# The cosine product of the rotated heads gets a tile of its own

## The chip, the cores and the metric

The kernel runs on one core of a Trainium2 chip. What counts is the device time of one execution in microseconds (us). The kernel before was timed three times: median 1780.94 us, lowest 1780.46, highest 1782.49. The execution that was profiled took 1781.29 us, of which 1779.5 us are the profile's span.

## The reference

Two layers of an encoder over 512 tokens and 1024 channels, all in float32. Each layer runs three token mixers side by side (differential attention, a convolution module, a neighbourhood attention), merges them through gates, and adds a feed-forward part and a gated input embedding. The change lies in the differential attention, whose queries and keys are first turned by a rotary embedding:

```python
def apply_rope(x, cos, sin):
    half = x.shape[-1] // 2
    x1, x2 = x[..., :half], x[..., half:]
    rot = jnp.concatenate([-x2, x1], axis=-1)
    return (x.astype(jnp.float32) * cos + rot.astype(jnp.float32) * sin).astype(x.dtype)

# diff_attention, 4 heads of 2 x 64 channels
q = apply_rope(q, cos, sin)
k = apply_rope(k, cos, sin)
s = jnp.einsum('bhcqd,bhckd->bhcqk', qi, k).astype(f32) * scale
a = jax.nn.softmax(s, axis=-1)
a = (a[:, :, 0] - lam * a[:, :, 1]).astype(v.dtype)
o = jnp.einsum('bhqk,bhkd->bhqd', a, v)
```

## The kernel before

Channels lie on the 128 partitions, the 512 tokens along the free axis. Every float32 product is made of three TensorE (PE) products of a high and a low part: ScalarE (ACT) copies an operand to the high part, VectorE (DVE) subtracts it to get the low part (`split`; its two instructions stand at L143 and L157, the lines of the helpers `act` and `tt`). Weights come as 512 KB tiles by transfers that SyncE (SP) issues (L171), and are split the same way into tiles `wh` and `wl`.

A stage is named by the first word of a tile: `natten` the neighbourhood attention, `diff` the differential attention, `gatec` the gates that are projected between its heads, `conv` the convolution, whose 31 taps per channel block (L160, tile `conv_z`) are slipped into DVE's order one by one after given instructions (`background`).

In the differential attention `diff_in` runs once for each of four heads, and in it once for the query (s=0) and once for the key (s=1). PE projects the head into PSUM. ACT copies it to a tile `raw`. Four transfers (L814) on SP's queue copy `raw` to a tile `rot` with the two halves of each 64 channels exchanged. DVE multiplies `raw` by the cosine table in place, `rot` by the sine table in place (whose sign is folded in), and adds. The sum is split: the high part goes to `kh`, the low part to `raw` itself, seen as another type. Transfers at L664 then stack both parts on partitions for the score products (`stack`). `raw` and `rot` both come from the pool tag `rp`, and both show as `diff_rp` in the profile; the cosine and sine tables show as `diff_r`. One convolution tap follows the cosine product (`bg["diff"]` is 1).

The scores of one head come in four units of 128 queries (`diff_unit`, `probs`). Each unit makes two score tiles `sc` in PSUM, one for each half of the differential head, each by two matmuls at L796. For each, DVE takes the maximum (L888) and ACT the exponential (into a tile `a` for the first, `e` for the second). There are two PSUM buffers for `sc`, so the second score tile of a unit can be written only when the exponential of the second tile of the unit before has been taken. I call the two score tiles of a unit a pair. The first pair of head 0 lies near 168 us of the span in the first layer and near 1049 us in the second.

PE's order is written out by the program. The order of the other engines' instructions (DVE, ACT, SP and the rest) is set by a scheduler when the kernel is built: it places each instruction where it expects its operands to be ready, and each engine then runs its list strictly in order, an instruction that waits holding up all that stand behind it.

## Time and profile before

| | |
|---|---|
| median of 3 runs | 1780.94 us (1780.46 to 1782.49) |
| profiled execution | 1781.29 us, span 1779.5 us |
| PE busy | 1764.2 us, 99% of the span |
| DVE busy | 1362.5 us, 77% |
| ACT busy | 900.6 us, 51% |
| transfers on SP's queue (q1) | 227.83 MB, 41.8% of 16 engines' span |

The views used below: the page; the waits (who waited for whom); the chain of waits, which is followed back from the last instruction and printed in order of time as start, duration, what; the timeline of one engine (start, duration, engine, line, operation, tile written <- tiles read, and in square brackets the idle time ahead of the instruction with what ended it); the groups by line (busy time, mean ns of one, idle time ahead with its cause); and the table of windows, which gives the busy time of each engine and the clock granted to PE in a stretch of the span. In the timeline a matmul's duration overlaps the next one's; how fast PE goes is read from the distance of starts.

### The profile page before, as it was taken

The numbers are of one execution on the slowest core, as the hardware profiler recorded it, in microseconds if no ns is written. First come the engines' busy times: TensorE is split into PE (matmuls) and PEld (weight loads), VectorE is DVE, ScalarE is ACT, GpSimd is POOL, SyncE is SP. The second block draws the span as 40 slices with busy tenths as digits, with TensorE's granted clock in tenths as the row PEclk, the third lists the DMA queues.
The fourth block names the chain that finished last, engine by engine and source line by source line (L and its number), as shares of the span: only waits on it lengthen the run. The fifth ranks groups of instructions, "written<-read, shape, count | busy, mean of one in ns | idle before, by whom it ended". The sixth has DMA issues, their size and how long they took to land.

```text
span 1779.5 us, 27113 instructions
## 1 busy us (share of the span) xinstructions
PE 1764.2 (99%) x10146; PEld 1555.6 (87%) x10146; DVE 1362.5 (77%) x2220; ACT 900.6 (51%) x1559; POOL 103.8 (6%) x114
## 2 busy tenths in 40 slices
PE   9999999999999999999999999999999999999998
PEld 7888888888899899998888888888888998989987
DVE  7867887998787576777776678889887865766676
ACT  5566545325576254454545655452356652634544
POOL 0000000000121010100000000000001210101000
PEclk9999999999999999999999999999999999999999
DMA  6575541334767365543536645423256664655332
GB/s 231 157 196 148 156 126 43 112 98 144 225 158 184 116 164 155 141 120 127 159 126 171 194 133 148 113 71 95 94 177 197 173 177 113 175 140 154 99 104 95
DMA packets 114787, 253.95 MB, mean 143 GB/s; under 512 B 16864, under 2 KB 23776, under 8 KB 114656
## 3 DMA queue, kind: packets, MB, share of 16 engines
q1 hardware_dynamic: 101264, 227.83, 41.8%
q0 software_dynamic: 12672, 23.07, 7.9%
q8 instruction: 80, 1.31, 0.3%
q10 hardware_dynamic: 720, 1.31, 0.2%
q14 instruction: 51, 0.42, 0.1%
HBM read 215.46 MB, written 7.34 MB: 125 GB/s over the span
## 4 chain that ended last, share of the span: by engine, by line
PE 92%; ACT 3%; DVE 2%; DMA 2%; issue 1%; SPq 0%; POOL 0%; ACTq 0%; POOLq 0%; DVEq 0%
PE ffn_mm L177 4%; PE ffn_mm L178 4%; PE ffn_mm L179 4%; PE ffn_mm L1005 3%; PE ffn_mm L1003 3%; PE ffn_mm L1004 3%; PE ffn_sc L1003 3%; PE ffn_sc L1004 3%; PE ffn_sc L1005 3%; PE mergea_mm L178 2%; PE mergea_mm L177 2%; PE mergea_mm L179 2%; PE gateb_mm L178 2%; PE gateb_mm L177 2%; PE gateb_mm L179 2%; PE wo_mm L177 2%
## 5 line engine op out<-in xcount | busy, mean ns | idle before, releaser
L160 DVE SCALAR_TENSOR_TENSOR conv_z<-glu_z,pre_par,conv_z 128x512 f32<-128x512 f32 x240 | 179.6, 748 | 3.4
L143 ACT ACTIVATE ffn_wh<-ffn_wr 128x1024 fp32r<-128x1024 f32 (+1 forms) x92 | 93.4, 1021 | 141.2 <-PE ffn_mm L178 76.0
L157 DVE TENSOR_TENSOR ffn_wl<-ffn_wr,ffn_wh 128x1024 fp32r<-128x1024 f32 (+1 forms) x92 | 107.6, 1175 | 41.2 <-ACT ffn_wh L143 40.9
L973 POOL DMA_DIRECT2D ffn_qk<-w_fu x88 | 77.8, 963 | 601.6 <-DMA ffn_qk<-w_fu 266.2
L157 DVE TENSOR_TENSOR ffn_t<-ffn_mm,wo_rb 128x512 f32<-128x512 f32 (+1 forms) x86 | 47.8, 557 | 71.7 <-PE ffn_mm L179 61.4
L143 ACT ACTIVATE mergea_wh<-mergea_wr 128x1024 fp32r<-128x1024 f32 (+1 forms) x32 | 27.1, 846 | 96.8 <-PE mergea_mm L178 79.5
L157 DVE TENSOR_TENSOR ffn_wl<-ffn_qk,ffn_wh 128x1024 fp32r<-128x1024 f32 x44 | 53.9, 1224 | 15.2 <-ACT ffn_wh L143 15.2
L143 ACT ACTIVATE ffn_wh<-ffn_qk 128x1024 fp32r<-128x1024 f32 x44 | 46.6, 1059 | 33.0 <-PE ffn_mm L178 16.2
L143 ACT ACTIVATE diff_a<-diff_sc,diff_s 128x512 f32<-128x512 f32 x32 | 21.9, 685 | 59.9 <-DVE diff_s L888 59.9
L177 PE MATMUL ffn_mm<-ffn_v,ffn_wh 128*128 128x512 f32 x132 | 51.4, 389 | 0.0
L178 PE MATMUL ffn_mm<-ffn_v,ffn_wh 128*128 128x512 f32 x132 | 51.4, 389 | 0.0
L179 PE MATMUL ffn_mm<-ffn_v,ffn_wl 128*128 128x512 f32 x132 | 51.3, 389 | 0.0
L177 PE MATMUL ffn_mm<-ffn_y,ffn_wh 128*128 128x512 f32 x132 | 51.3, 389 | 0.0
L178 PE MATMUL ffn_mm<-ffn_y,ffn_wh 128*128 128x512 f32 x132 | 51.3, 389 | 0.0
L179 PE MATMUL ffn_mm<-ffn_y,ffn_wl 128*128 128x512 f32 x132 | 51.3, 389 | 0.0
L1003 PE MATMUL ffn_mm<-wo_h,ffn_wh 128*128 128x256 f32 x176 | 49.9, 284 | 0.0
L1004 PE MATMUL ffn_sc<-wo_h,ffn_wh 128*128 128x256 f32 x176 | 49.8, 283 | 0.0
L1005 PE MATMUL ffn_mm<-wo_h,ffn_wl 128*128 128x256 f32 x176 | 49.8, 283 | 0.0
L1005 PE MATMUL ffn_sc<-wo_h,ffn_wl 128*128 128x256 f32 x176 | 49.8, 283 | 0.0
L1003 PE MATMUL ffn_sc<-wo_h,ffn_wh 128*128 128x256 f32 x176 | 49.8, 283 | 0.0
L1004 PE MATMUL ffn_mm<-wo_h,ffn_wh 128*128 128x256 f32 x176 | 49.8, 283 | 0.0
L143 ACT ACTIVATE natten_wh<-natten_wr 128x1024 fp32r<-128x1024 f32 x24 | 25.4, 1058 | 42.1 <-issue 15.2
(861 smaller groups left out, 6490.7 us busy)
## 6 DMA issues: line engine op xcount, KB each, us to landing
ffn_qk<-w_fu POOLq DMA_DIRECT2D x88, 256.0 KB, 6.2
ffn_wr<-w_fg SPq DMA_DIRECT2D x44, 512.0 KB, 4.8
ffn_wr<-w_fd SPq DMA_DIRECT2D x32, 448.0 KB, 4.1
ffn_r<-w_fu SPq DMA_DIRECT2D x44, 256.0 KB, 3.3
ffn_qk<-w_fg SPq DMA_DIRECT2D x44, 256.0 KB, 2.9
ffn_qk<-w_fu SPq DMA_DIRECT2D x44, 256.0 KB, 3.2
natten_wr<-w_in SPq DMA_DIRECT2D x16, 512.0 KB, 4.4
diff_wr<-w_in SPq DMA_DIRECT2D x16, 512.0 KB, 3.8
```

The source lines that it names most:

```text
L143: i = self.nc.scalar.activation(out, in_, func, **kw)
L157: return self.nc.vector.tensor_tensor(out, a, b, op)
L160: return self.nc.vector.scalar_tensor_tensor(out, a, s, b, op0, op1)
L177: mm(out, wh, ah, start=first, stop=False, **kw)
L178: mm(out, wh, al, start=False, stop=False, **kw)
L179: mm(out, wl, ah, start=False, stop=last, **kw)
L973: nc.gpsimd.dma_start(q, wu[:, lo], accum_op=ALU.add)
L1003: mm(out, wh[:, c], bh, start=first and k == 0, stop=False, skip_group_check=True)
L1004: mm(out, wh[:, c], bl, start=False, stop=False, skip_group_check=True)
L1005: mm(out, wl[:, c], bh, start=False, stop=k == 3, skip_group_check=True)
```

## The change

The cosine product is written to a new tile `t` from the pool tag `t` (seven buffers, used by other stages too) and no longer over `raw`. The sum is made in `t`, and the split reads `t`. The low part still goes to `raw`.

```diff
             for b in range(4):
                 o = b ^ 1
                 self.nc.sync.dma_start(rot[32 * b:32 * b + 32], raw[32 * o:32 * o + 32])
-            self.background(self.tt(raw, raw, st["tabs"][0], ALU.mult), self.bg["diff"])
+            t = self.sb("t", [P, 512])
+            self.background(self.tt(t, raw, st["tabs"][0], ALU.mult), self.bg["diff"])
             self.tt(rot, rot, st["tabs"][1], ALU.mult)
-            self.tt(raw, raw, rot, ALU.add)
+            self.tt(t, t, rot, ALU.add)
             nat, low = self.sb("kh", [P, 512], F32R), raw.bitcast(F32R)
-            self.split(nat, low, raw)
+            self.split(nat, low, t)
             self.stack(nat, low, st4[:, 2 * s:2 * s + 2], k2 if s else None)
```

The number of instructions and transfers stays as it was. The lists of PE and GpSimd (POOL) are the same before and after; those of DVE, ACT and SP differ inside the differential stage, in the same way in both layers. Because the diff adds a line, L888 is L889 in the changed kernel, and L893 is L894. The number at the end of a tile's name only tells instances apart.

DVE, first layer, query of head 1, in the kernel before (`diff_rp_1742` is `raw`, `diff_rp_1743` is `rot`, `diff_r_1321` the cosine and `diff_r_1323` the sine table, `diff_sc_1808` and `diff_sc_1814` the two score tiles of head 0's first pair):

```order
L157 TENSOR_TENSOR natten_y_1320<-natten_av_1779,natten_y_1320 64x512
L157 TENSOR_TENSOR natten_pt_1796<-natten_tr_1791,natten_pt_1796 128x512
L157 TENSOR_TENSOR natten_y_1320<-natten_y_1320,natten_av_1779 64x512
L157 TENSOR_TENSOR natten_pt_1804<-natten_tr_1799,natten_pt_1804 128x512
L888 TENSOR_REDUCE diff_s_1807<-diff_sc_1808 128x1
L157 TENSOR_TENSOR diff_rp_1742<-diff_rp_1742,diff_r_1321 128x512
L160 SCALAR_TENSOR_TENSOR conv_z_370<-glu_z_321,pre_par_67,conv_z_370 128x512
L157 TENSOR_TENSOR diff_rp_1743<-diff_rp_1743,diff_r_1323 128x512
L157 TENSOR_TENSOR diff_wl_2007<-diff_wr_2005,diff_wh_2006 128x1024
L157 TENSOR_TENSOR diff_rp_1742<-diff_rp_1742,diff_rp_1743 128x512
L888 TENSOR_REDUCE diff_s_1807<-diff_sc_1814 128x1
L157 TENSOR_TENSOR diff_rp_1742<-diff_rp_1742,diff_kh_1753 128x512
```

The same place in the changed kernel (`diff_rp_1744` is `raw`, `diff_rp_1745` is `rot`, `diff_t_1751` the new tile):

```order
L157 TENSOR_TENSOR diff_t_1751<-diff_rp_1744,diff_r_1321 128x512
L160 SCALAR_TENSOR_TENSOR conv_z_370<-glu_z_321,pre_par_67,conv_z_370 128x512
L157 TENSOR_TENSOR natten_y_1320<-natten_av_1782,natten_y_1320 64x512
L157 TENSOR_TENSOR natten_pt_1799<-natten_tr_1794,natten_pt_1799 128x512
L157 TENSOR_TENSOR natten_y_1320<-natten_y_1320,natten_av_1782 64x512
L157 TENSOR_TENSOR natten_pt_1807<-natten_tr_1802,natten_pt_1807 128x512
L889 TENSOR_REDUCE diff_s_1810<-diff_sc_1811 128x1
L157 TENSOR_TENSOR diff_rp_1745<-diff_rp_1745,diff_r_1323 128x512
L889 TENSOR_REDUCE diff_s_1810<-diff_sc_1817 128x1
L157 TENSOR_TENSOR diff_t_1751<-diff_t_1751,diff_rp_1745 128x512
L157 TENSOR_TENSOR diff_wl_2012<-diff_wr_2010,diff_wh_2011 128x1024
L894 RECIPROCAL diff_s_1810<-diff_s_1810 128x1
```

The cosine product and its tap have moved ahead of six instructions, and the maximum of the second score tile stands directly behind the sine product, ahead of the sum and the split of a weight tile.

ACT at the same place, before (`diff_rp_1835` is `raw` of head 1's key, `diff_kh_1753` the high part of head 1's query, `diff_e_1818` the exponential of the second score tile):

```order
L143 ACTIVATE diff_a_1812,diff_sm_1502<-diff_sc_1808,diff_s_1807 128x512
L143 ACTIVATE diff_wh_2006<-diff_wr_2005 128x1024
L143 ACTIVATE diff_rp_1835<-diff_mm_1760 128x512
L143 ACTIVATE diff_kh_1753<-diff_rp_1742 128x512
L143 ACTIVATE diff_e_1818,diff_s_1807<-diff_sc_1814,diff_s_1807 128x512
L143 ACTIVATE natten_y_1320<-natten_mm_1877 64x512
```

and now:

```order
L143 ACTIVATE diff_a_1815,diff_sm_1504<-diff_sc_1811,diff_s_1810 128x512
L143 ACTIVATE diff_wh_2011<-diff_wr_2010 128x1024
L143 ACTIVATE diff_e_1821,diff_s_1810<-diff_sc_1817,diff_s_1810 128x512
L143 ACTIVATE diff_kh_1756<-diff_t_1751 128x512
L143 ACTIVATE diff_rp_1838<-diff_mm_1763 128x512
L143 ACTIVATE natten_y_1320<-natten_mm_1881 64x512
```

The exponential of the second score tile now stands ahead of the query's high part, and the copy of head 1's key to `raw` behind it.

SP's queue from the rotating transfers of head 1's query on, before (`diff_rp_1836` is `rot` of the key, `diff_qk_1693` the stacked query and key):

```order
L814 DMA diff_rp_1743<-diff_rp_1742 32x512 x3
L814 DMA diff_rp_1836<-diff_rp_1835 32x512
L171 DMA diff_wr_2277<-w_in 128x1024
L664 DMA diff_qk_1693<-diff_kh_1753 64x512 x2
L664 DMA diff_qk_1693<-diff_rp_1742 64x512 x2
L814 DMA diff_rp_1836<-diff_rp_1835 32x512 x3
```

and now:

```order
L814 DMA diff_rp_1745<-diff_rp_1744 32x512 x3
L664 DMA diff_qk_1695<-diff_kh_1756 64x512 x2
L664 DMA diff_qk_1695<-diff_rp_1744 64x512 x2
L171 DMA diff_wr_2283<-w_in 128x1024
L814 DMA diff_rp_1839<-diff_rp_1838 32x512 x4
```

All four rotating transfers of the key now stand behind the query's stacking transfers and a weight tile's load; before, one of the four stood ahead of them.

## The prediction

> **What bounds the kernel now.** The page comes first:

> ```profile
> PE 1764.2 (99%) x10146; PEld 1555.6 (87%) x10146; DVE 1362.5 (77%) x2220; ACT 900.6 (51%) x1559; POOL 103.8 (6%) x114
> PE 92%; ACT 3%; DVE 2%; DMA 2%; issue 1%; SPq 0%; POOL 0%; ACTq 0%; POOLq 0%; DVEq 0%
> ```

> PE is busy for 99% of the span, and PE's list is not changed. So only the time in which PE stands still or goes slowly can move. The waits of PE say where it stands still (engine, line, what it waited for, us in total, times, longest):

> ```profile
> PE diff_sc L796 <- ACT diff_e L143: 6.2, 2, 3.8
> PE ffn_mm L1005 <- DVE ffn_pt L157: 2.0, 2, 1.0
> PE pre_av L327 <- DVE pre_zeror L400: 1.1, 1, 1.1
> ```

> The largest, two waits of 6.2 us together, lies in the score products of the differential stage, beside the changed lines. PE's timeline shows the two places, one per layer, each the second score tile of head 0's second pair:

> ```profile
> 175.60 0.40 PE L796 MATMUL diff_sc<-diff_x,diff_qk 128*128 128x512 f32 x1
> 178.46 0.50 PE L796 MATMUL diff_sc<-diff_qk 128*128 128x512 f32 x1 [2.46 <-ACT diff_e L143]
> 1056.21 0.40 PE L796 MATMUL diff_sc<-diff_x,diff_qk 128*128 128x512 f32 x1
> 1060.38 0.79 PE L796 MATMUL diff_sc<-diff_qk 128*128 128x512 f32 x1 [3.77 <-ACT diff_e L143]
> ```

> What ACT and DVE did meanwhile is in the chain of waits (start, duration, what):

> ```profile
> 169.91 3.27 DMA diff_rp<-diff_rp
> ...
> 173.90 0.75 DVE conv_z L160
> 174.65 0.60 DVE diff_rp L157
> 175.25 1.14 DVE diff_wl L157
> 176.39 0.61 DVE diff_rp L157
> ...
> 177.02 0.63 ACT diff_kh L143
> 177.65 0.76 ACT diff_e L143 x2
> ...
> 178.46 0.72 PE diff_sc L796 x2
> ```

> The exponential that frees PE's buffer stands on ACT behind the query's high part, which needs the rotated sum, which stands on DVE behind a weight split, the sine product, a tap and the cosine product, which waits for the rotating transfers to have read its tile. The second layer has the same chain, with a later landing: its DVE row is

> ```profile
> 1055.22 0.69 DVE L157 TENSOR_TENSOR diff_rp<-diff_rp,diff_r 128x512 f32<-128x512 f32 x1 [3.27 <-DMA diff_rp<-diff_rp]
> ```

> A wait costs more than itself. The table of windows (stretch, its length, busy us of PE, PEld, DVE, ACT, POOL, PE's clock, DMA share, GB/s) and the chain show PE at half clock behind both waits, and at full clock behind the wait of 1.0 us in the feed-forward stage:

> ```profile
> 180.00:182.00 2.00, 2.00 (x6) 1.56 (x5) 1.91 (x4) 0.78 (x2) 0.00 (x0) 0.50 0.77 248
> 1062.00:1064.00 2.00, 2.00 (x7) 1.57 (x6) 1.91 (x4) 0.78 (x2) 0.00 (x0) 0.55 0.73 240
> 522.00:524.00 2.00, 2.00 (x19) 2.00 (x18) 1.13 (x3) 1.30 (x3) 0.30 (x1) 1.00 1.05 236
> 183.50 0.23 PE diff_mm L177
> 1064.07 0.23 PE gatec_mm L177
> ```

> **What can be won.** In the first layer the waiting matmul would have started 0.23 us (the step of the last rows above) after 175.60, at 175.83; it started 2.63 late. From 178.46 to 183.50 the chain has 14 matmuls of 512 columns, 5.04 us, where 14 x 0.227 = 3.17 would do: 1.87. In the second layer: due 1056.44, late by 3.94; 8 matmuls from 1060.38 to 1064.07 take 3.69 against 1.81: 1.88. So the first layer holds 4.50 us, the second 5.82, together **10.3 us**. More than that the change cannot give.

> [...]

> **The change part by part.** Nothing is added in number: the cosine product with another output tile stays the same 128x512 operation, priced by its group (busy, mean ns | idle ahead):

> ```profile
> L157 DVE TENSOR_TENSOR diff_rp<-diff_rp,diff_r 128x512 f32<-128x512 f32 x32 | 21.9, 686 | 6.3 <-DMA diff_rp<-diff_rp 6.3
> ```

> The same product into another tile has no row; the nearest is the weight split, which writes a tile of its own and takes 1.23 us for 1024 columns (row below), 0.61 for 512. So the change of target costs between -0.07 and 0 us, 16 times; I take 0, and on DVE, idle for a quarter of the span, even 1.1 us in all would not reach PE's end. The new tile takes a buffer of tag `t`. Seven allocations earlier, for head 1's query, lies a tile of the gated convolution input, long read, so that no wait comes with it.

> What moves is the order. I walk the first layer with the starts of the trace:

> ```profile
> 166.68 1.23 DVE L157 TENSOR_TENSOR diff_wl<-diff_wr,diff_wh 128x1024 fp32r<-128x1024 f32 x1 [0.26 <-ACT diff_wh L143]
> 170.64 0.68 DVE L888 TENSOR_REDUCE diff_s<-diff_sc 128x1 f32<-128x512 f32 x1
> 173.29 0.69 DVE L157 TENSOR_TENSOR diff_rp<-diff_rp,diff_r 128x512 f32<-128x512 f32 x1 [1.97 <-DMA diff_rp<-diff_rp]
> 166.54 0.60 ACT L143 ACTIVATE diff_rp<-diff_mm 128x512 f32<-128x512 f32 x1
> ```

> 1. `raw` is there at 167.14, so the cosine product and its tap follow the weight split (ends 167.91) at once; in the chain above DVE's instructions start 0.61 to 0.75 us apart, so these two push the four `natten` splits and the first maximum back by 1.3 us, from 170.64 to about 171.95. That maximum then ends near 172.6, before the rotating transfers land at 173.2. DVE had idled 1.97 us there (3.27 in the second layer); this idle time is the cover of the two moved instructions.
> 2. SP's rotating transfers of the query keep their places, so they land as before, and the sine product starts at 173.29. Its tile is the one that now waits; behind it on DVE queue the second maximum, the sum and a weight split.
> 3. The second maximum starts 0.61 later, at 173.90, and ends at 174.58. ACT has copied the weight tile by then (1.05 us from about 173.3) and takes the exponential at once: with its accumulator read it needs 0.81 us until PE starts (177.65 to 178.46 above), so the buffer is free at about 175.45. PE wants it at 175.83: **no wait, 0.4 us to spare**.
> 4. In the second layer the same steps start 1055.22 - 173.29 = 881.93 later: free at 1057.38, wanted at 1056.44, **0.94 us of wait left**, below the 1.0 that kept full clock.
> 5. What is late next is the following pair, since PE now comes earlier:

> ```profile
> 186.53 0.39 PE L796 MATMUL diff_sc<-diff_qk 128*128 128x512 f32 x1
> 1068.43 0.39 PE L796 MATMUL diff_sc<-diff_qk 128*128 128x512 f32 x1
> ```

> From the sine product to its release DVE and ACT have in the new order: sine, maximum and sum (3 x 0.61), weight split (1.13), reciprocal, small product (2 x 0.25), low part, cosine of the key, difference of exponentials, tap, maximum, `natten` split, maximum (7 x 0.68), exponential (0.81): 9.03 us. The release is at 182.32 and 1064.25; PE wants it at 186.53 - 4.50 = 182.03 and 1068.43 - (5.82 - 0.94) = 1063.55. Left: **0.29 and 0.70 us**.
> 6. The key of head 1 is copied on ACT behind the query's high part, at about 176.5, and its four transfers stand behind the query's stack and a weight load on SP. The rows that say whether that is in time:

> ```profile
> 180.14 1.86 SPq L814 DMA_DIRECT2D diff_rp<-diff_rp  x3
> DMA to landing us min/median/max: 1.9/2.9/5.4
> 195.91 1.25 SPq L664 DMA_DIRECT2D diff_x<-diff_rp  x2
> diff_x<-diff_rp SPq DMA_DIRECT2D x16, 128.0 KB, 2.6
> 201.26 0.40 PE L796 MATMUL diff_sc<-diff_qk 128*128 128x512 f32 x1
> ```

> Now the last three transfers are issued by 182.00. In the new order the four follow the query's high and low part (ready at 176.1 and 177.2 by step 5), four stacking transfers and one load of about 0.6 us each, so the last is issued at about 181.2 and lands by 186.6 at the latest. The sine product, standing behind the third pair's maxima, starts at about 186, the stack is issued 7.7 us later at about 193.7 (now 197.16) and lands after 2.6 more at 196.3. PE's first pair of head 1 moves from 201.26 to 197.1. Cover: 0.8 us. I take nothing for it; at the longest landing it would be late by about 2.

> A PE that is 4 to 5 us ahead needs a DVE that can follow:

> ```profile
> 220.00:240.00 20.00, 20.00 (x105) 16.95 (x104) 16.43 (x30) 11.70 (x24) 0.00 (x0) 1.00 0.50 140
> 260.00:280.00 20.00, 20.00 (x107) 17.10 (x106) 13.66 (x23) 8.90 (x17) 0.00 (x0) 1.00 0.13 39
> 300.00:320.00 20.00, 20.00 (x99) 16.79 (x98) 19.77 (x32) 6.03 (x9) 1.44 (x1) 1.00 0.40 119
> ```

> DVE's 3.6 and 6.3 us of idle time in the first two windows let it do so before it is full at 300 us. The rest of the moves (cosines of heads 0, 2 and 3 ahead, loads shifted on SP) I cost at nothing: PE waits for none of these tiles in its list of waits, and 3 us of later load stay inside the 5 us that one weight tile lasts PE (24 matmuls of 0.227).

> **The sum.** 10.3 less what is left: 0.94 + 0.29 + 0.70 = 1.9, so 8.4 us; I take **8 us**. The profiled execution (1781.29) would be 1773.3. The runs' median is 0.35 lower, so about **1773.0 us**. All hangs on half-microseconds in steps 3 to 5: with 0.5 us against me in each of the four places, still below the wait at which the clock fell, the gain is 6; with 0.5 us in my favour it is near 10. That gives the likeliest case 1771 to 1775.

> **The rivals.**

> *The wait shrinks but keeps its clock loss.* The landings of the rotating transfers spread from 1.9 to 5.4 us. If the second layer's is a microsecond later, or the first maximum delays the exponential, 1.5 to 2 us of wait stay there. A wait of 2.46 us halved the clock and one of 1.0 did not; in between no row tells. Then that layer gives 3.94 - 2 = 1.9 or less, the first about 2.5 to 4.5: 3 to 6 us, 1775 to 1778. For it speaks that the second maximum still stands behind an instruction that waits for the landing; against it the 0.4 us to spare in the first layer.

> *The wait only moves.* PE catches up with DVE at the next pair or at head 1's stack and stands there as long: then the tap and the cosine ahead of the first maximum have only reordered a DVE-bound stretch. DVE between 173 and 187 has almost no idle time in the new order, which speaks for it; but the walk over these instructions leaves only 0.3 to 0.7. It would be 1781, within the 0.2% (3.5 us) that a measurement of this kernel can tell from none. The same comes if the cosine product waits for its new tile instead.

> *The key of head 1 comes too late.* Its rotation now stands behind the query's stack and a 512 KB load on SP. The load takes

> ```profile
> diff_wr<-w_in SPq DMA_DIRECT2D x16, 512.0 KB, 3.8
> ```

> If the rotation queues behind another such load, it lands at 186.6 + 3.8 = 190.4 and the stack, 7.7 us of work and 2.6 of flight later, at 200.7; if the stack meets one too, at 204.5. PE then stands 3.6 to 7.4 us from 197.1 on, plus 1.9 of clock, in both layers: 11 to 18.6 lost against 8 won, 1784 to 1792; I take 1787. It decides once the stack lands after 199.2 (4.0 us won per layer less 1.9 of clock, from 197.1). Against it: the trace's stacks land 2.6 us after issue, and DVE reaches the sine product only at 186 anyhow.

> **How the numbers follow.** Forecast 0.62, shrinking wait 0.20, moved wait 0.11, late key 0.07. Faster by over 0.2% (below 1777.4) takes the forecast and nearly all of the second, 0.80; within 0.2%: 0.13; slower: 0.07. The range runs from 1770.3 (all 10.3, and the spread of the runs) to 1780.5, which takes in the shrinking wait and part of the moved one.

> **What would show it.** The two waits of PE at 178 and 1060 gone or below 1 us, with granted clock 1.00 behind them; DVE idle ahead of the sine product rather than the cosine product; the second maximum directly behind it and the exponential ahead of the high part; new waits of at most a microsecond at the third pair, in the second layer above all. Wrong would be: the clock at 0.5 anywhere near 180 or 1060, or a wait of over 2 us at a pair of head 0 or at head 1's first.

## The result and the profile after

The changed kernel takes 1770.89 us (median of 4 runs, 1770.37 to 1771.12) where the kernel before takes 1781.43 (4 runs, 1780.46 to 1782.49): a ratio of 0.9941, with a 95% interval of 0.9928 to 0.9953, or 10.5 us less. The forecast was 1773.0 in a range of 1770.3 to 1780.5. The profiled execution took 1770.93 us with a span of 1769.2, 10.3 below that of before.

The busy times on the page of the changed kernel:

```profile
PE 1760.0 (99%) x10146; PEld 1553.3 (88%) x10146; DVE 1361.1 (77%) x2220; ACT 900.6 (51%) x1559; POOL 104.0 (6%) x114
```

PE's 10146 matmuls are busy 4.2 us less (1764.2 before), though none was taken away; the busy times of DVE, ACT and POOL stay within 1.4 us. PE's list of waits in the changed kernel (us in total, times, longest) begins with what was second and third before:

```profile
PE ffn_mm L1006 <- DVE ffn_pt L157: 2.0, 2, 1.0
PE pre_av L327 <- DVE pre_zeror L400: 1.1, 1, 1.1
```

The row of 6.2 us for `diff_sc` is gone and no row has come in its place. PE's timeline of the changed kernel shows the same score tiles, none with a wait in brackets: the second tile of the second pair (175.20 and 1051.25) and of the third (181.58 and 1057.63; its first is at 181.13), and the first tile of the fourth pair (188.37 and 1064.55) and of head 1's first pair (196.31):

```profile
175.20 0.39 PE L796 MATMUL diff_sc<-diff_qk 128*128 128x512 f32 x1
...
181.13 0.39 PE L796 MATMUL diff_sc<-diff_qk 128*128 128x512 f32 x1
...
181.58 0.39 PE L796 MATMUL diff_sc<-diff_qk 128*128 128x512 f32 x1
...
188.37 0.39 PE L796 MATMUL diff_sc<-diff_qk 128*128 128x512 f32 x1
...
196.31 0.40 PE L796 MATMUL diff_sc<-diff_qk 128*128 128x512 f32 x1
...
1051.25 0.40 PE L796 MATMUL diff_sc<-diff_qk 128*128 128x512 f32 x1
...
1057.63 0.50 PE L796 MATMUL diff_sc<-diff_qk 128*128 128x512 f32 x1
...
1064.55 0.39 PE L796 MATMUL diff_sc<-diff_qk 128*128 128x512 f32 x1
```

The table of windows of the changed kernel, at the two places where the clock had been 0.50 and 0.55, gives 1.00 (it is the last but two of a row's numbers):

```profile
180.00:182.00 2.00, 2.00 (x10) 1.69 (x9) 1.77 (x5) 1.52 (x3) 0.00 (x0) 1.00 0.91 340
1057.00:1060.00 3.00, 3.00 (x14) 2.31 (x13) 2.80 (x6) 1.52 (x3) 0.00 (x0) 1.00 0.44 153
```

DVE's timeline of the changed kernel shows the new order. The cosine product and its tap run before the landing, ahead of the four `natten` splits and the first maximum (five instructions, not six as the section on the change counts), the idle time lies ahead of the sine product, and the second maximum follows it:

```profile
167.27 0.69 DVE L157 TENSOR_TENSOR diff_t<-diff_rp,diff_r 128x512 f32<-128x512 f32 x1
167.87 0.75 DVE L160 SCALAR_TENSOR_TENSOR conv_z<-glu_z,pre_par,conv_z 128x512 f32<-128x512 f32 x1
...
171.17 0.68 DVE L889 TENSOR_REDUCE diff_s<-diff_sc 128x1 f32<-128x512 f32 x1
172.65 0.69 DVE L157 TENSOR_TENSOR diff_rp<-diff_rp,diff_r 128x512 f32<-128x512 f32 x1 [0.80 <-DMA diff_rp<-diff_rp]
173.26 0.68 DVE L889 TENSOR_REDUCE diff_s<-diff_sc 128x1 f32<-128x512 f32 x1
...
1048.97 0.69 DVE L157 TENSOR_TENSOR diff_rp<-diff_rp,diff_r 128x512 f32<-128x512 f32 x1 [2.09 <-DMA diff_rp<-diff_rp]
```

On ACT, in the timeline of the changed kernel, the exponential now stands ahead of the query's high part:

```profile
173.98 0.69 ACT L143 ACTIVATE diff_e<-diff_sc,diff_s 128x512 f32<-128x512 f32 x1 [0.37 <-DVE diff_s L889]
174.57 0.19 ACT L143 ACTIVATION_READ_ACCUMULATOR diff_e<-diff_sc,diff_s 128x1 f32 x1
174.66 0.62 ACT L143 ACTIVATE diff_kh<-diff_t 128x512 fp32r<-128x512 f32 x1
```

**Where the time came from.** Executions come to the first `natten` product up to 0.9 us apart (at 112.64 to 113.56 us in the nine traces), so I read distances inside one execution. PE's timeline of before, from the first `natten` product near 113 us to head 0's fourth pair, over the place near 156 us that is spoken of below, and from the first to the fourth pair in the second layer:

```profile
112.84 0.48 PE L177 MATMUL natten_mm<-glu_h,natten_wh 128*128 128x512 f32 x1
...
155.44 0.28 PE L621 MATMUL diff_mm<-diff_wh,glu_h 128*128 128x256 f32 x1
155.90 0.36 PE L796 MATMUL natten_sc<-natten_qk 128*128 128x256 f32 x1 [0.18 <-PE diff_mm L621]
...
157.12 0.40 PE L177 MATMUL diff_mm<-glu_h,diff_wh 128*128 128x512 f32 x1
...
193.32 0.39 PE L796 MATMUL diff_sc<-diff_qk 128*128 128x512 f32 x1
...
1048.60 0.48 PE L796 MATMUL diff_sc<-diff_qk 128*128 128x512 f32 x1
...
1075.22 0.39 PE L796 MATMUL diff_sc<-diff_qk 128*128 128x512 f32 x1
```

and the same rows of the changed kernel (the fourth pairs stand above):

```profile
112.86 0.48 PE L177 MATMUL natten_mm<-glu_h,natten_wh 128*128 128x512 f32 x1
...
155.46 0.28 PE L621 MATMUL diff_mm<-diff_wh,glu_h 128*128 128x256 f32 x1
155.58 0.28 PE L796 MATMUL natten_sc<-natten_qk 128*128 128x256 f32 x1
...
156.54 0.40 PE L177 MATMUL diff_mm<-glu_h,diff_wh 128*128 128x512 f32 x1
...
1043.39 0.48 PE L796 MATMUL diff_sc<-diff_qk 128*128 128x512 f32 x1
```

First layer: 193.32 - 112.84 = 80.48 before, 188.37 - 112.86 = 75.51 now, 4.97 less. Second: 1075.22 - 1048.60 = 26.62 before, 1064.55 - 1043.39 = 21.16 now, 5.46 less. Together 10.4, the whole of the span's 10.3. I call these two distances the first and the second layer's stretch from here on. Of the first, 0.60 comes from a place that the prediction didn't have: the eight `natten` score products near 156 us took 157.12 - 155.44 = 1.68 us, and now take 156.54 - 155.46 = 1.08.

### The profile page after: what moved, and what is told of

Its sections match the earlier page's. It is cut to its first block, busy times and chain, and to the rows that moved or that the text cites. A ratio compares the mean times of both kernels' runs of the same rounds, so it can differ in the third digit from the quotient of the medians.

```text
span 1769.2 us, 27111 instructions
## 1 busy us (share of the span) xinstructions
PE 1760.0 (99%) x10146; PEld 1553.3 (88%) x10146; DVE 1361.1 (77%) x2220; ACT 900.6 (51%) x1559; POOL 104.0 (6%) x114
## 4 chain that ended last, share of the span: by engine, by line
PE 98%; DVE 1%; ACT 1%; issue 0%; POOL 0%; POOLq 0%; ACTq 0%; DVEq 0%
PE ffn_mm L177 4%; PE ffn_mm L178 4%; PE ffn_mm L179 4%; PE ffn_mm L1006 3%; PE ffn_mm L1004 3%; PE ffn_mm L1005 3%; PE ffn_sc L1004 3%; PE ffn_sc L1005 3%; PE ffn_sc L1006 3%; PE mergea_mm L177 2%; PE mergea_mm L179 2%; PE mergea_mm L178 2%; PE diff_sc L796 2%; PE diff_mm L177 2%; PE diff_mm L178 2%; PE gatec_mm L178 2%
## 5 line engine op out<-in xcount | busy, mean ns | idle before, releaser
L160 DVE SCALAR_TENSOR_TENSOR conv_z<-glu_z,pre_par,conv_z 128x512 f32<-128x512 f32 x240 | 179.6, 748 | 3.4
L143 ACT ACTIVATE ffn_wh<-ffn_wr 128x1024 fp32r<-128x1024 f32 (+1 forms) x92 | 93.3, 1021 | 141.8 <-PE ffn_mm L178 76.6
L157 DVE TENSOR_TENSOR ffn_wl<-ffn_wr,ffn_wh 128x1024 fp32r<-128x1024 f32 (+1 forms) x92 | 107.6, 1175 | 41.3 <-ACT ffn_wh L143 40.9
L157 DVE TENSOR_TENSOR ffn_t<-ffn_mm,wo_rb 128x512 f32<-128x512 f32 (+1 forms) x86 | 47.8, 557 | 72.2 <-PE ffn_mm L179 61.9
L143 ACT ACTIVATE mergea_wh<-mergea_wr 128x1024 fp32r<-128x1024 f32 (+1 forms) x32 | 27.1, 846 | 96.8 <-PE mergea_mm L178 79.6
L157 DVE TENSOR_TENSOR ffn_wl<-ffn_qk,ffn_wh 128x1024 fp32r<-128x1024 f32 x44 | 53.9, 1224 | 15.2 <-ACT ffn_wh L143 15.2
L143 ACT ACTIVATE ffn_wh<-ffn_qk 128x1024 fp32r<-128x1024 f32 x44 | 46.6, 1059 | 33.0 <-PE ffn_mm L178 16.2
L143 ACT ACTIVATE diff_a<-diff_sc,diff_s 128x512 f32<-128x512 f32 x32 | 22.0, 688 | 71.1 <-DVE diff_s L889 71.1
L177 PE MATMUL ffn_mm<-ffn_v,ffn_wh 128*128 128x512 f32 x132 | 51.4, 389 | 0.0
L177 PE MATMUL ffn_mm<-ffn_y,ffn_wh 128*128 128x512 f32 x132 | 51.3, 389 | 0.0
L1005 PE MATMUL ffn_sc<-wo_h,ffn_wh 128*128 128x256 f32 x176 | 49.8, 283 | 0.0
L1005 PE MATMUL ffn_mm<-wo_h,ffn_wh 128*128 128x256 f32 x176 | 49.8, 283 | 0.0
L143 ACT ACTIVATE natten_wh<-natten_wr 128x1024 fp32r<-128x1024 f32 x24 | 25.4, 1058 | 42.1 <-issue 15.2
## 6 DMA issues: line engine op xcount, KB each, us to landing
ffn_wr<-w_fg SPq DMA_DIRECT2D x44, 512.0 KB, 4.4
natten_wr<-w_in SPq DMA_DIRECT2D x16, 512.0 KB, 4.4
diff_wr<-w_in SPq DMA_DIRECT2D x16, 512.0 KB, 4.2
```

The costliest lines, as they stand in the source:

```text
L143: i = self.nc.scalar.activation(out, in_, func, **kw)
L157: return self.nc.vector.tensor_tensor(out, a, b, op)
L160: return self.nc.vector.scalar_tensor_tensor(out, a, s, b, op0, op1)
L177: mm(out, wh, ah, start=first, stop=False, **kw)
L1005: mm(out, wh[:, c], bl, start=False, stop=False, skip_group_check=True)
```

## The experiments

The first four runs are compared with one set of runs of the kernel before (22 runs, median 1780.71 us), the last three with another (19 runs, 1781.23). Behind each run stand the two stretches against those of before. From the second experiment on, the diffs are against the changed kernel.

### Only the order, the cosine product still in place

The cosine product of head 1's query is put behind the second maximum by an order given to the scheduler. It still writes over `raw`.

```diff
-            self.background(self.tt(raw, raw, st["tabs"][0], ALU.mult), self.bg["diff"])
+            cos = self.tt(raw, raw, st["tabs"][0], ALU.mult)
+            self.background(cos, self.bg["diff"])
+            if head == 1 and s == 0:
+                self.late = cos
...
-            nc.vector.tensor_reduce(out=m[:, u:u + 1], in_=sc, op=ALU.max, ...)
+            top = nc.vector.tensor_reduce(out=m[:, u:u + 1], in_=sc, op=ALU.max, ...)
+            if u and self.late is not None:
+                self.behind(self.late, top)
+                self.late = None
```

> The kernel before, cosine product in place as it was; only, in each layer, the cosine product of head 1's query is ordered behind the second maximum of head 0's first pair. On DVE the sine product (which waits for the same landing) then comes first, the second maximum behind it, the cosine product third; on ACT the exponential stands ahead of head 1's high part. Theory A (what counts is that the exponential which frees PE's buffer no longer stands behind the rotation; the new tile only led the scheduler to that order): the two waits of 2.46 and 3.77 us fall below 1 us and the clock stays at 1.00 behind them; the cosine product now costs its 0.6 us on the way to the third pair, so that 0.5 to 1.5 us of wait come back there; 5 to 9 us faster than before, 1773 to 1776. Theory B (the cosine product and its tap must be done before the landing, which only a tile of its own allows): the waits shrink by at most 1.4 us each and the half clock stays; 0 to 3 us faster.

Measured: 1775.18 us (1774.84 to 1776.26), ratio 0.997 (0.9959 to 0.9982), 5.5 us less than before; the stretches 4.03 and 3.01 shorter. PE waits for `diff_e` three times, 2.2 us together; its timeline has them at the first layer's third pair and at the second layer's second and third:

```profile
183.05 0.50 PE L796 MATMUL diff_sc<-diff_qk 128*128 128x512 f32 x1 [0.43 <-ACT diff_e L143]
...
1054.14 0.50 PE L796 MATMUL diff_sc<-diff_qk 128*128 128x512 f32 x1 [0.89 <-ACT diff_e L143]
...
1061.91 0.50 PE L796 MATMUL diff_sc<-diff_qk 128*128 128x512 f32 x1 [0.88 <-ACT diff_e L143]
```

What it shows: the order alone, with no new tile, removes the long waits and brings the clock back (a mean of 1.000 over this execution, 0.997 before). That is half of the gain by the times (5.5 us, with an interval of 3.2 to 7.3) and two thirds by the stretches of the one traced execution (7.04 of 10.43). Of the 3.4 us by which its stretches are longer than those of the changed kernel, 1.9 lie at the third pairs, where the cosine product and its tap now stand between the landing and the release. 1.3 lie at the second layer's second pair, where the landing comes as late as before (step 4 below), and 0.2 near 156 us. DVE's timeline of this run has the cosine product still behind the landing:

```profile
173.11 0.69 DVE L157 TENSOR_TENSOR diff_rp<-diff_rp,diff_r 128x512 f32<-128x512 f32 x1 [1.54 <-DMA diff_rp<-diff_rp]
...
174.32 0.68 DVE L157 TENSOR_TENSOR diff_rp<-diff_rp,diff_r 128x512 f32<-128x512 f32 x1
```

From the sine product to the third pair's second tile it takes 183.05 - 173.11 = 9.94 us here and 9.93 in the second layer, against 181.58 - 172.65 = 8.93 and 8.66 in the changed kernel: 1.0 and 1.3 more, for two instructions (0.60 and 0.66 from start to start). In the first layer of the changed kernel PE, not the release, set that end, as step 5 below shows.

### The tile of its own, but the cosine product held behind the sine product

```diff
             t = self.sb("t", [P, 512])
-            self.background(self.tt(t, raw, st["tabs"][0], ALU.mult), self.bg["diff"])
-            self.tt(rot, rot, st["tabs"][1], ALU.mult)
+            sin = self.tt(rot, rot, st["tabs"][1], ALU.mult)
+            cos = self.tt(t, raw, st["tabs"][0], ALU.mult)
+            self.behind(cos, sin)
+            self.background(cos, self.bg["diff"])
```

> The changed kernel with the cosine product in its own tile, but ordered behind the sine product, so that it waits for the landing again; ACT has the old order (high part ahead of the exponential). Theory A: as before the change, 1780 to 1783, with waits of 2.3 to 4 us at the second pair and the half clock behind them. Rival (not waiting on the tile that the transfers read is worth something by itself): at least half of the gain is kept, 1776 or less.

Measured: 1781.34 us (11 runs, 1778.74 to 1783.3), ratio 1.0006 (0.9997 to 1.0015): no gain. The stretches are 1.46 shorter and 0.73 longer: the wait in the first layer cost no clock this time (6.04 us to the third pair, 7.62 before); the table further below compares it with the others. PE's timeline has both waits again:

```profile
179.14 0.50 PE L796 MATMUL diff_sc<-diff_qk 128*128 128x512 f32 x1 [2.30 <-ACT diff_e L143]
...
1059.69 0.79 PE L796 MATMUL diff_sc<-diff_qk 128*128 128x512 f32 x1 [3.58 <-ACT diff_e L143]
```

and ACT's timeline of this run again has the exponential behind the high part that waits for the sum:

```profile
177.71 0.63 ACT L143 ACTIVATE diff_kh<-diff_t 128x512 fp32r<-128x512 f32 x1 [3.30 <-DVE diff_t L157]
178.31 0.69 ACT L143 ACTIVATE diff_e<-diff_sc,diff_s 128x512 f32<-128x512 f32 x1
```

So the tile by itself is worth nothing that can be measured here. What pays is the place in the order that it permits.

### The tile of its own for head 1's query alone

```diff
-            t = self.sb("t", [P, 512])
+            t = self.sb("t", [P, 512]) if head == 1 and s == 0 else raw
```

> The change made for the query of head 1 alone (2 of the 16 rotations); all others in place. Theory A (nearly all of the gain is that one rotation, whose wait sits in front of the exponential): 9 to 10 us faster than before; only the 0.4 to 0.8 us that PE loses near 156 us, behind head 0's key, comes back. Rival (each rotation gives its share, 10.5/8 us for one head's query in both layers): 1 to 3 us faster.

Measured: 1771.9 us (1770.88 to 1772.36), ratio 0.995 (0.9938 to 0.9963), 8.8 us less, a little under the 9 to 10 expected, which the interval (6.6 to 11.0) takes in; the stretches 4.33 and 5.29 shorter, and no wait of PE for `diff_e`. One rotation of eight in each layer carries some 85% of the gain. The 0.60 us near 156 us is not won here: head 0's first pair comes 55.12 us after the `natten` product (55.13 before). From the sine product to the third pair's second tile it takes 8.64 us in the second layer, as in the full change, with the other seven rotations in place.

### The first layer alone

```diff
-            t = self.sb("t", [P, 512])
+            t = self.sb("t", [P, 512]) if self.i == 0 else raw
```

> The change made in the first layer alone. Theory A: the layers are independent; the first gives 4.5 to 5.0 us, so 1776.4 to 1777.0, and the second keeps its wait of about 3.8 us with the half clock. Rival (a PE that is 5 us ahead from the first layer on waits them off elsewhere, and only both together count): under 3 us.

Measured: 1777.16 us (11 runs, 1776.21 to 1778.74), ratio 0.9979 (0.997 to 0.9988), 3.6 us less. In the trace the first layer's stretch is 4.97 shorter, to the hundredth that of the full change. The second layer's is 0.84 longer than before: its wait is the same (3.65 against 3.77) but PE went slowly for longer behind it, 8.55 us from the second pair's second tile to the third pair against 7.60. So in the trace the first layer gives what was computed, and the longer stretch of half clock in the second takes some of it back; the table further below sets it beside the others. The traced execution, at 1778.74 us, was the slowest of the eleven. Their median misses the 4.5 to 5.0 us expected by a microsecond, but its interval, 2.1 to 5.3, takes them in, so that no more can be told from the times.

### The key of head 0 alone

This is the place of the 0.60 us near 156 us, without the rotation on which the rest hangs.

```diff
-            t = self.sb("t", [P, 512])
+            t = self.sb("t", [P, 512]) if head == 0 and s == 1 else raw
```

> The change made for the key of head 0 alone. Theory A (the 0.6 us that the changed kernel had won ahead of head 0's first pair come from a PE wait of 0.2 us near 156 us, at the neighbourhood scores, which stand behind head 0's key on DVE): that wait is gone, head 0's first pair is reached 0.5 to 0.7 us earlier, and the run is 0.4 to 1 us faster, which the runs can hardly tell from none. The waits of 2.5 and 3.8 us at the second pair stay. Rival: the 0.6 us come from another place, and the wait near 156 us stays.

Measured: 1779.32 us (11 runs, 1777.74 to 1781.9), ratio 0.9991 (0.9982 to 0.9999), 1.9 us less, at the edge of what can be told. Head 0's first pair comes 167.46 - 112.97 = 54.49 us after the `natten` product, against 167.97 - 112.84 = 55.13 before: the 0.6 us is the key's. But the first layer's stretch is 2.72 shorter, far more than that (the second's 0.15). PE's timeline shows why:

```profile
177.45 0.50 PE L796 MATMUL diff_sc<-diff_qk 128*128 128x512 f32 x1 [1.97 <-ACT diff_e L143]
```

The wait shrank by half a microsecond, from 2.46 to 1.97, and with it the whole clock loss behind it went: the third pair follows after 183.49 - 177.45 = 6.04 us, not 7.62. The 1.6 us belonged to this wait, and not to head 0's key. The cosine product, which waits for the rotating transfers, started 172.29 - 167.46 = 4.83 us after the first pair, where it was 173.29 - 167.97 = 5.32 before; whether the edit did that or a shorter flight of the transfers (the time from issue to landing) isn't shown. The half microsecond was not foreseen, and led to the next two runs.

### The wait put back in doses

The full change, with copies of the exponential ahead of the one that frees the buffer, in head 0's first pair: one in the first layer and two in the second, then two and three. They leave the result as it is and delay PE by ACT's time: by 0.65 us from two copies to three (2.02 and 2.67 us of wait, below).

```diff
+            self.more = True
...
+            if u and self.more:
+                self.more = False
+                for _ in range((1,2)[i]):
+                    self.act(e, sc, AF.Exp, table="exp", bias=m[:, u:u + 1])
```

> The changed kernel with the second exponential of head 0's first unit taken 2 times in the first layer and 3 times in the second (the same instruction again, its output overwritten), to make PE wait by a chosen amount. With the high part slipping in between, the buffer comes free about 1.2 and 2.3 us later; with 0.4 and 0.15 us to spare PE waits about 0.8 and 2.1 us. Theory C (a wait under 1 us costs only itself, one above some bound between 1.0 and 2.46 us halves the clock for about 3.5 us more and costs 1.9 us extra): the first layer loses 0.8 us at clock 1.00; the second 2.1 us, or 4.0 if the bound lies below 2.1. Rival (the extra cost grows with the wait from zero on): the first loses 1.2 to 1.5.

> As the run before, with 3 exponentials in the first layer and 4 in the second. PE waits about 1.85 and 2.75 us. Theory C: the second layer loses 2.75 + 1.9 = 4.6 us; the first 1.85, or 3.7 if the bound lies below 1.85.

Measured: 1774.17 us (1771.83 to 1774.81), ratio 0.9957 (0.9944 to 0.9969), for one and two copies; 1777.35 (1775.86 to 1779.29), ratio 0.9977 (0.9967 to 0.9987), for two and three. The stretches are 3.74 and 3.30 shorter than before with one and two copies, 2.65 and 1.02 with two and three. The waits came out at 0.62 and 2.02, and at 2.06 and 2.67 us. Against the change, the first layer with one copy lost 1.23 us, the figure of the rival; but the clock stayed at 1.00 there, and 0.34 of it lies behind the third pair, so this was not a clock loss that grows with the wait. The second layer of each, PE's timeline and the window behind it, first with two copies:

```profile
1055.20 0.50 PE L796 MATMUL diff_sc<-diff_qk 128*128 128x512 f32 x1 [2.02 <-ACT diff_e L143]
```

```profile
1057.00:1059.00 2.00, 2.00 (x11) 1.65 (x10) 1.92 (x3) 0.53 (x1) 0.00 (x0) 1.00 1.00 211
```

then with three:

```profile
1056.39 0.50 PE L796 MATMUL diff_sc<-diff_qk 128*128 128x512 f32 x1 [2.67 <-ACT diff_e L143]
```

```profile
1058.00:1060.00 2.00, 2.00 (x6) 1.51 (x6) 1.91 (x4) 0.67 (x3) 0.00 (x0) 0.50 0.77 294
```

With 0.65 us more of wait the clock is halved. All waits at this place, from the traces of all the kernels, by the time from the waiting matmul to the first matmul of the third pair (the column in the middle is explained below):

| idle ahead of it, us | most of it in one frame, us | kernel, layer | to the third pair, us |
|---|---|---|---|
| none | | the change, first and second | 5.93, 5.92 |
| 0.62 | 0.62 | one and two copies, first | 6.05 |
| 0.89 | 0.89 | only the order, second | 6.16 |
| 1.97 | 1.12 | key of head 0, first | 6.04 |
| 2.02 | 1.62 | one and two copies, second | 6.03 |
| 2.06 | 1.07 | two and three copies, first | 6.04 |
| 2.30 | 1.55 | cosine behind sine, first | 6.04 |
| 2.46 | 2.11 | before, first | 7.62 |
| 2.67 | 2.67 | two and three copies, second | 7.66 |
| 3.58 | 2.12 | cosine behind sine, second | 8.51 |
| 3.65 | 2.29 | first layer alone, second | 8.55 |
| 3.68 | 3.41 | key of head 0, second | 7.52 |
| 3.77 | 3.39 | before, second | 7.60 |

Against 5.93 us without a wait, those of 0.62 to 2.30 us cost themselves and 0.1 to 0.2 more, those of 2.46 to 3.77 themselves and 1.6 to 2.6 more. The length of the wait alone does not tell what is lost: 3.58 and 3.65 us cost 2.6 more, 3.68 and 3.77 only 1.6 and 1.7. The table of windows, cut into quarters of a microsecond, shows when the clock fell and rose: in the kernel before, in both layers,

```profile
179.75:180.00 0.25, 0.25 (x2) 0.21 (x1) 0.25 (x1) 0.00 (x0) 0.00 (x0) 0.53 1.01 221
183.00:183.25 0.25, 0.25 (x2) 0.21 (x1) 0.00 (x0) 0.00 (x0) 0.00 (x0) 0.64 0.04 8
1060.25:1060.50 0.25, 0.12 (x1) 0.12 (x1) 0.19 (x2) 0.23 (x2) 0.00 (x0) 0.81 1.03 426
1063.75:1064.00 0.25, 0.25 (x2) 0.21 (x2) 0.24 (x1) 0.08 (x1) 0.00 (x0) 0.86 0.21 66
```

and in the second layer with the cosine product behind the sine product:

```profile
1058.00:1058.25 0.25, 0.00 (x0) 0.00 (x0) 0.25 (x2) 0.00 (x0) 0.00 (x0) 0.96 0.00 0
1065.00:1065.25 0.25, 0.25 (x2) 0.21 (x1) 0.00 (x0) 0.00 (x0) 0.00 (x0) 0.89 0.00 0
```

In the kernel before, the windows of 0.25 us ahead of and behind these two stretches read 1.00, and all those inside read 0.50. With one step between the two values, 0.53 over 0.25 us means that the clock was halved for 94% of them, so it fell at 179.765. In the same way it rose at 183.18, fell and rose at 1060.405 and 1063.82, and at 1058.23 and 1065.055. The half clock thus lasted 3.41 us, 3.41, and 6.83, which is twice as long. The two falls of the kernel before lie 880.64 us apart, 258 times 3.4133. The same execution has a third at its end, where PE has no more work (0.91 over 1777.00 to 1777.25, so at 1777.205), 716.80 us or 210 times 3.4133 behind the second. Three other executions have a second fall at their end; it lies 211 times 3.4133 us behind the one in the table (first layer alone, at 1055.11 and 1775.325) and 210 times (key of head 0, 1057.24 and 1774.035; two and three copies, 1057.06 and 1773.855). So in these four executions the falls lay on a grid of 3.41 us, over 717 to 1597 us. I call one step of it a frame.

The column in the middle of the table lays this grid over the waits. For the six losses it is counted back from the fall itself. For the waits that kept the clock it is an estimate, in steps of 3.4133 us from another fall of the same execution (1058.23, 1057.24 and 1057.06; for the two executions without a fall in the table, the one at their end, 1771.60 and 1771.875). The waits with up to 1.62 us in one frame left the clock at 1.00; those with 2.11 us or more had it halved at the end of the frame. The wait of 2.30 us, which kept the clock, was cut by a border of the estimated grid into 0.75 and 1.55; that of 3.58 lost it at 1058.23, when PE had stood for only 2.12 us. The half clock lasted two frames (6.83 us) where the frame behind the fall held another 1.36 or 1.46 us of idle time (3.65 and 3.58), and one (3.41 us) where it held 0.24 or less. How the borders fall differs between executions: in the first layer they lay 8.38 and 11.80 us behind head 0's first pair before, 9.14 and 12.55 with the key of head 0. So by this estimate the step between 2.30 and 2.46 is chance, and what sets the two groups of these traces apart is the idle time in a frame: 1.62 us and less, 2.11 and more.

## Why the prediction was right, and where its steps were not

**What can be won: 10.3 us, close to the measured 10.5, but with luck.** The sum is made of other parts than reckoned: the two places gave 9.8, and 0.6 came from a place that the prediction had at nothing, against its sentence that the change cannot give more. The first layer's clock loss moreover was that of one execution; with another place of the grid the same wait of 2.46 us would have been cut in two and, by the estimate under the table, could have kept the clock. That the loss belongs to the wait is shown by the doses: in the changed kernel a wait of 2.67 us brought it back, and waits of 2.02 and 2.06 did not.

**Steps 1 and 2, right in the first layer.** The group by line of the changed kernel prices the product into its own tile:

```profile
L157 DVE TENSOR_TENSOR diff_t<-diff_rp,diff_r 128x512 f32<-128x512 f32 x16 | 10.9, 682 | 0.0
```

682 ns against 686 in place. The first maximum came at 171.17; with the 0.64 us by which this stretch runs ahead (first pair 167.33 against 167.97) that is 171.81 for 171.95. The sine product came at 172.65, or 173.29 on the clock of before: the very number of step 2.

**Step 3, right.** ACT's accumulator read ends at 174.76 and PE wanted the buffer at 175.20: 0.4 us to spare, as computed. With one copy of the exponential the spare time is used up and 0.62 of wait is seen.

**Step 4, wrong: 0.94 us of wait in the second layer, none measured.** The step took the second layer's landing as far behind its pair as before. It was not. The product that waits for the landing, the sine now and the cosine before, starts 1048.97 - 1043.39 = 5.58 us after head 0's first pair, against 1055.22 - 1048.60 = 6.62. SP's timeline of the changed kernel has the last three rotating transfers at

```profile
1042.85 1.80 SPq L814 DMA_DIRECT2D diff_rp<-diff_rp  x3
```

and that of before at

```profile
1048.98 1.81 SPq L814 DMA_DIRECT2D diff_rp<-diff_rp  x3
```

that is 0.54 us ahead of the first pair now and 0.38 behind it before, 0.92 us earlier. ACT split the weight tile whose buffer the load between them needs 0.9 us earlier too (1040.07, 3.32 ahead of the pair, against 1046.19, 2.41 ahead); that this is the cause is argued, not shown. So 0.92 of the 1.04 came from an earlier issue, the rest from the flight. The experiment with only the order is the check on the step itself: there the landing kept its place (1051.98 - 1045.23 = 6.75) and the wait was 0.89, as step 4 has it. With head 1's query alone the landing came after 5.90 without an earlier issue, by a shorter flight (3.70 us from the end of the last issue, 1055.22 - 1050.79 = 4.43 before). So that no wait was left in the second layer is luck as far as the step goes: the landing that it took as fixed moves by up to a microsecond. Why flights of the same four transfers differ by half a microsecond stays open.

**Step 5, mis-sized: 9.03 us from the sine product to the release, 8.64 measured.** In the second layer the third pair's second tile starts at 1057.63, 8.66 behind the sine product, and PE wanted it at 1057.62 (1057.17 and twice 0.227): met without a wait. In the first layer the release came 8.64 behind, at 181.29, and PE wanted it at 181.58, so 0.3 was to spare where 0.29 of wait was forecast. The waits of 0.29 and 0.70 in the sum are the term that was too large: by 0.39 in the release, of which 0.29 are the reciprocal and the small product (0.08 and 0.13 us on DVE from start to start, taken as 2 x 0.25), by 0.19 in the first layer because PE gained 4.31 us there and not 4.50, and in the second by what step 4 had missed.

**Step 6, right.** The key's rotating transfers and the query's stack are the next two rows of SP's timeline of the changed kernel:

```profile
178.45 2.44 SPq L814 DMA_DIRECT2D diff_rp<-diff_rp  x4
...
191.13 1.25 SPq L664 DMA_DIRECT2D diff_x<-diff_rp  x2
```

They end at 180.89 and 192.38, and head 1's first pair runs at 196.31 without a wait. On the clock of before, 0.64 later, that is 181.53, 193.02 and 196.95, where 181.2, 193.7 and 197.1 were forecast.

**The sum.** Forecast: 10.3 less 0.94, 0.29 and 0.70, rounded to 8. Measured: nothing of the three came, and the span lost 10.3. So the forecast of 1773.0 was 2.1 us too high, and 1770.89 lies just outside its likeliest case of 1771 to 1775 and 0.6 above the lower end of its range. The stretches show it as 4.97 and 5.46, which is 9.8 at the places of the sum and 0.60 near 156 us. The 9.8 is the two late starts, 2.63 and 3.94, and a clock loss of 1.69 and 1.68 (7.62 less 5.93 and 7.60 less 5.92, where 14 and 8 matmuls had been reckoned as 1.87 and 1.88), less 0.1 at the third pair of the second layer. The 0.60 near 156 us was missing altogether. It is seen in a row of before that I passed over, for a `natten` product with 0.18 us in brackets. The run with the key of head 0 alone shows that its rotation holds PE there. Part of it comes and goes with the landing: with only the order, the key's cosine product was still in place but found its transfers landed (it started 149.38 - 142.12 = 7.26 us after the weight split ahead of it, against 149.15 - 141.44 = 7.71), and the eight products took 157.35 - 156.12 = 1.23 us. That the key holds PE through DVE, which empties the `natten` score tiles a microsecond earlier in the new order, is argued from the timelines and not shown.

**The rivals.** *The wait shrinks but keeps its clock loss* did not happen in the changed kernel. It took 1.5 to 2 us of wait as enough to halve the clock; 1.97 to 2.30 did not in four cases, but by the estimated grid one with 2.11 us in one frame could have. In four of the six losses of the table PE was at work for 0.7 to 1.3 us of the frame at whose end the clock fell. *The wait only moves*: the experiment with only the order shows it in small, with 0.43 and 0.88 at the third pair; with the tile it would take 0.3 us more in the first layer and nothing more in the second to bring it on. *The key of head 1 comes too late*: its stack landed in time, with all four transfers behind the load.

## What to carry to other kernels

The operation in place over the tile that the transfers were reading kept DVE idle for 1.97 and 3.27 us until they had landed, and held up all that stood behind it in DVE's list; a spare tile paid only where the operation could then move into idle time ahead of the landing (1.0006 without the move, 0.9941 with it), and a better order alone gave half or more. Price a stall of TensorE by its length and by the clock behind it: here six stalls of 2.46 to 3.77 us cost 1.6 to 2.6 us more than themselves and six of 0.62 to 2.30 at most 0.2 more, and where the grid of the clock lay differed between executions, so one traced execution is one draw. And one rotation out of eight held nearly all of it, so look for the instance beside the stall before you count all of them.

## What the runs showed of the hardware

The times fit this: the 22 runs of before spread over 4.4 us (1778.57 to 1782.96), the 4 of the changed kernel, which has no such stall, over 0.75. That the grid makes this spread isn't shown, since one execution of each kernel was traced.

The four rotating transfers of head 1's query landed (the product that waited for them started) 3.70 to 4.57 us after the end of their last issue in the second layer, with only head 1's query and with the key of head 0 as the ends, and 1.73 to 2.81 in the first: enough to make or unmake a wait of half a microsecond.
